# Three edits in an fp32 transformer trunk: first blocks that leave two k-tiles to the end, the sigmoid ahead of the squares, values in thirds of 344 columns

## The chip, the cores and the metric

The kernel runs on one core of a Trainium2 chip. The time is device microseconds of one execution, and a kernel's time is the median over several. TensorE (PE) multiplies matrices, VectorE (DVE), ScalarE (ACT) and GpSimd (POOL) work element by element, and SyncE (SP) issues nearly all transfers. Each engine takes its instructions strictly in the order in which the program gives them to it.

## The reference

Two layers over 256 tokens of width 1024. A layer is a half-step SwiGLU feed-forward, a token mixer, a second half-step SwiGLU, and a gated embedding; layer 0 mixes with latent attention (MLA), layer 1 with forgetting attention (FoX). Cut to what matters here:

```python
for i in range(DEPTH):
    h = h + 0.5 * swiglu(rms_norm(h, ffn_norm[i, 0]), ffn_w_in[i, 0], ffn_w_out[i, 0])
    u = rms_norm(h, mix_norm[i])
    h = h + (mla_mixer(u, ...) if i % 2 == 0 else fox_mixer(u, ...))
    h = h + 0.5 * swiglu(rms_norm(h, ffn_norm[i, 1]), ffn_w_in[i, 1], ffn_w_out[i, 1])
    gate = sigmoid(rms_norm(h, ple_norm[i]) @ ple_w_gate[i])
    h = h + gate * (p[i] @ ple_w_proj[i])
return rms_norm(h, final_norm)
# fox_mixer: q, k, v (8 heads of 128) and 8 forget logits f = u @ w_in;
# scores = q k^T / sqrt(128) + cum_q - cum_k with cum = cumsum(log_sigmoid(f + b)); causal softmax; @ w_o
```

## The kernel before, in words

Activations are kept transposed: `hT` (in the tile `state`) has 8 k-tiles of 128 features by 256 tokens. All operands of a product are split into a high and a low part (`whi`, `wlo` for weights, a pair `u` for activations), and a product is three partial ones. A feed-forward block for one k-tile is therefore two matmuls: one of 512 columns (line 235: high weights against both parts) and one of 256 (line 236: low weights against the high part). A block has 8 k-tiles.

**Weights.** The class `Weights` walks one list of tiles, `plan`. `fetch` has SP load tiles up to four ahead of the last finished one. `high` (line 97) has ACT make `whi`, `low` (line 101) has DVE make `wlo`, a 128x1024 subtraction. `pump` finishes one tile, `catch_up` pumps only if fewer than four tiles are finished ahead of those handed out (`loaded < got + 4`), and `get` hands out. Where a pump stands in the program decides where its line-101 subtraction stands among DVE's other instructions.

**Norms.** While a stage finishes its eight output tiles, the next stage's operand is built from each: `high` (line 275, ACT; line 273, DVE for the last), `low` (line 280, DVE), `square` (line 286, ACT) and a running sum of the squares `acc` (line 291, POOL). `by_token` and `by_column` turn the sum into scale factors later: two small matmuls (`pst`), a DVE operation `v`, a power on POOL (`rtok`), and two more small matmuls (`pb`). The products run on the unscaled operand, so a stage can begin before its scale is known.

**First blocks.** `blocks` starts a stage on the first k-tiles of two blocks. Before the change it runs seven k-tiles of the gate block `pg`, seven of the up block `pu`, and then the eighth of each. It is used at the start of three feed-forwards (after MLA, after the gated embedding, after FoX) and at the start of MLA.

**Gated embedding** (`ple`, between layer 0 and layer 1). For each of 8 tiles d, PE makes `ps`; DVE scales it (`zg`, line 792); ACT makes the sigmoid `sg` (line 793); DVE makes `low` of tile d-1 (line 280), perhaps a weight's `wlo` (line 101), the product `ge` (line 801) and the new `state` (line 802); ACT makes `high` and `square` of tile d, and POOL adds the square to `acc`.

**FoX.** First come the values, with the 8 forget logits beside them: four column groups `pv`, the first 264 wide, the others 256 wide, each for two token halves, 8 k-tiles and 3 partial products (lines 220 to 222). `by_token`, `by_column` and the forget gate's steps (`gates`) hang on fixed places in that loop. Then `attention` runs its heads as a pipeline: in round h it makes the shares of head h-2 (`inv`, `pr`, lines 447 to 449, DVE), the two projections of head h (`ps`, then `two` and `kqv`, lines 757 and 758), turns head h-2 (`pt`, line 455, PE), scores head h-1 (`psc`) and multiplies head h-2's values (`po`, line 462). A `catch_up` follows the second projection. From round 8 on there are no projections, and PE fills in with the output product on as many k-tiles as the table `FOX_FILLS` says.

Of the kernel before, what the change touches and what calls it, by code (L numbers as in the profile page):

```python
# [15 lines left out]
AF = mybir.ActivationFunctionType  # L16
# [3 lines left out]
P = 128  # L20
D = 1024
T = 256
KD = D // P
FF = 2816
KF = FF // P
H = 8
# [12 lines left out]
G_Q = 72  # L39
G_KV = 74  # L40
GAINS = 80


MLA_FILLS = {(7, 1): 2, (8, 0): 4, (8, 1): 4, (9, 0): 4, (9, 1): 4, (10, 0): 3, (10, 1): 3}
# [94 lines left out]

@with_exitstack  # L140
def trunk(ctx, tc, xT, xt, pT, pos, freq, bf, lead0, lead1, ffn_in, ffn_out, w_down, w_uq, w_ukv, mla_o,
          fox_qk, fox_v, fox_f, fox_o, ple_gate, ple_proj, ple_rows, gain_row, out):
    nc = tc.nc
    const = ctx.enter_context(tc.tile_pool(name="const", bufs=1))
    wp = ctx.enter_context(tc.tile_pool(name="wp", bufs=1))
# [7 lines left out]
    plan = []  # L153
# [18 lines left out]
    plan_ffn(1)  # L172
    plan_ple()
    plan_ffn(2)
    plan.extend(fox_f[c] for c in range(2))
    plan.extend(fox_v[c] for c in range(KD - 2))
    plan.extend(fox_qk[c] for c in range(2 * H))
    plan.extend(fox_o[d] for d in range(KD))
    plan_ffn(3)
# [3 lines left out]

    state = const.tile([P, GAINS + KD * T], F32, name="state")
    g_sb, hT = state[:, :GAINS], state[:, GAINS:].rearrange("p (k t) -> p k t", k=KD)

# [15 lines left out]
    def tmp(name):  # L202
        return work.tile([P, T], F32, name=name, tag="tmp", bufs=5)

    def bank(name, shape=(P, 2, T)):
        return psum.tile(list(shape), F32, name=name, tag="mm")

    W = Weights(nc, wp, plan)
# [43 lines left out]
    def blocks(ps, x):  # L252

        ws = W.get(len(ps))
        for ks in (range(KD - 1), range(KD - 1, KD)):
            for p, w in zip(ps, ws):
                part(p, w, x, ks, KD - 1)
        W.done(*ws)
# [296 lines left out]
    def keys_values():  # L555

        kqv = big.tile([P, 2 * KF, T], F32, name="kqv", tag="big")
        return kqv[:, :24, :], kqv[:, 24:32, :].rearrange("p (t c) n -> p t (c n)", t=2)
# [110 lines left out]
    def fox(norm, nxt):  # L669
        kq, v = keys_values()  # L670
# [46 lines left out]
            nc.vector.tensor_copy(cumq, pc.rearrange("p t h -> p h t"))  # L717


        for c in range(4):  # L720
            w = W.get(2)
            n = T + H if c == 0 else T
            pv = [bank("pv0", (P, n)), bank("pv1", (P, n))]
            for k in range(KD):
                for t in range(2):
                    a = (k % 4) * n
                    mm3(pv[t], [norm.pair[:, k, u, t * P:(t + 1) * P] for u in range(2)],
                        [u[:, a:a + n] for u in w[k // 4][1:]], k == 0, k == KD - 1)
                if (c, k) == (0, KD - 2):
                    norm.by_token()  # L730
                elif (c, k) == (1, 3):
                    norm.by_column()
                elif (c, k) == (2, 2):
                    steps = gates()
                if steps:
                    next(steps, None)
                if k % 4 == 3:
                    W.done(w[k // 4])
                    if k == 3:
                        W.pump()  # L740
                        W.catch_up()
            for t in range(2):
                r = norm.rtok[:, t:t + 1]
                if c == 0:
                    nc.scalar.activation(zt[:, t, :].rearrange("p (j i) -> p j i", i=32)[:, :, :H],
                                         pv[t][:, T:].rearrange("p (o h) -> p o h", o=1).to_broadcast([P, 3, H]),
                                         AF.Copy, scale=r)
                nc.scalar.activation(v[:, t, c * T:(c + 1) * T], pv[t][:, :T], AF.Copy, scale=r)
            W.pump()

        def project(h, half):
            if (h, half) == (0, 1):
# [35 lines left out]
    def ple(pp, norm, nxt):  # L788
        def gated(d, z, e):
            zg, sg, ge = tmp("zg"), tmp("sg"), tmp("ge")  # L790
            src = hT[:, d, :]
            nc.vector.tensor_mul(zg, z, norm.rb)
            nc.scalar.activation(sg, zg, AF.Sigmoid)
            if d:
                nxt.low(d - 1, hT[:, d - 1, :])

            if d < 2:
                W.pump(2 - d)
            elif d < KD - 1:
                W.catch_up(3)  # L800
            nc.vector.tensor_mul(ge, e, sg)
            nc.vector.tensor_add(src, src, ge)
            if d < KD - 1:
                nxt.high(d, src)
                nxt.square(src)
            else:
                nxt.last(d, src)
                W.pump()


        es = big.tile([P, KD, T], F32, name="es", tag="big")
        for c in range(2):
            w, = W.get()
            for i in range(4):
                if i % 2 == 0:
                    pe = bank("pe")
                if (c, i) == (1, 3):
                    norm.by_column()
                part(pe[:, i % 2, :], w, pp, range(2), at=lambda k: k * 512 + i * P)
                if i % 2:  # L820
                    nc.scalar.activation(es[:, 4 * c + i - 1:4 * c + i + 1, :], pe, AF.Copy)
            W.done(w)
            if c == 0:
                norm.by_token()
            W.pump(2 - c)
        for d in range(KD):
            ps = bank("ps", (P, T))
            block(ps, norm.pair)
            gated(d, ps, es[:, d, :])
# [128 lines left out]
    for k in range(KD):  # L958
        if k % 2 == 0:
            hi, lo = W.pair()  # L960
        c = slice(k % 2 * 4 * P, (k % 2 + 1) * 4 * P)
        n0.high(k, steps[:, k, :T], vector=k == 0)

        n = 4 * P if k else 2 * P
# [145 lines left out]
    for i in range(2):  # L1110
# [6 lines left out]
        p = Embedding(i)  # L1117
# [9 lines left out]
def _cols(w, n):  # L1127

    k, m = w.shape
    return np.ascontiguousarray(w.reshape(k // P, P, m // n, n).transpose(2, 1, 0, 3)).reshape(m // n, P, -1)  # L1130


def _layout(x, p, positions, ffn_norm, ffn_w_in, ffn_w_out, mix_norm, mla_w_down, mla_q_norm, mla_w_uq,
            mla_kv_norm, mla_w_ukv, mla_w_o, fox_w_in, fox_b_f, fox_w_o, ple_norm, ple_w_gate,
            ple_w_proj, final_norm):
    a = {}
# [6 lines left out]

    g = np.concatenate([g.reshape(75, P).T, np.zeros((P, GAINS - 75), g.dtype)], axis=1)
    a["xT"] = np.ascontiguousarray(np.concatenate([g, xT], axis=1))
# [4 lines left out]
    w = ffn_w_in.reshape(4, KD, P, 2, KF, P)  # L1150
# [6 lines left out]
    w = ffn_w_out.reshape(4, KF, P, KD, P)  # L1157
    a["ffn_out"] = np.ascontiguousarray(w.transpose(0, 3, 2, 1, 4)).reshape(4, KD, P, KF * P)

    w = mla_w_down[0]  # L1160
    cq, ckv, kr = w[:, :256], w[:, 256:384], w[:, 384:]
    ks = np.concatenate([kr[:, 32:], kr[:, :32]], axis=1)
    a["w_down"] = _cols(np.concatenate([cq, ckv, kr, ks], axis=1), P)

    w = mla_w_uq[0].reshape(256, H // 2, 2, 192)
# [3 lines left out]
    w = np.concatenate([b.reshape(256, H // 2, -1) for b in (nope, rope)], axis=-1)  # L1169
    a["w_uq"] = _cols(w.reshape(256, -1), 512)  # L1170
    w = mla_w_ukv[0].reshape(P, H, 2, P)
    a["w_ukv"] = np.ascontiguousarray(w.transpose(2, 0, 1, 3)).reshape(2, P, D)
    a["mla_o"] = _cols(mla_w_o[0], P)
    w = fox_w_in[0]
    hd = H * P
    qk = w[:, :2 * hd].reshape(D, 2, H, P).transpose(0, 2, 1, 3).reshape(D, 2 * hd)
    a["fox_qk"] = _cols(qk, P)

    v = w[:, 2 * hd + T:3 * hd].reshape(2, KD // 2, P, 3, T)
    a["fox_v"] = np.ascontiguousarray(v.transpose(3, 0, 2, 1, 4)).reshape(KD - 2, P, D)  # L1180
    f = np.concatenate([w[:, 2 * hd:2 * hd + T], w[:, 3 * hd:]], axis=1).reshape(2, KD // 2, P, T + H)
    a["fox_f"] = np.ascontiguousarray(f.transpose(0, 2, 1, 3)).reshape(2, P, -1)
    a["fox_o"] = _cols(fox_w_o[0], P)
    a["ple_gate"] = _cols(ple_w_gate[0], P)

# [5 lines left out]


_ORDER = ["xT", "xt", "pT", "pos", "freq", "bf", "lead0", "lead1", "ffn_in", "ffn_out", "w_down", "w_uq", "w_ukv", "mla_o",
          "fox_qk", "fox_v", "fox_f", "fox_o", "ple_gate", "ple_proj",
          "ple_rows", "gain_row"]


# [18 lines left out]
```

## Time and profile before

| | |
|---|---|
| median of 3 runs | 1000.98 us (1000.59 to 1001.3) |
| the profiled execution | 1000.57 us, of which the span from first to last instruction is 998.8 us |
| PE | busy 988.1 us, 99% of the span |
| DVE, ACT, POOL | 74%, 52%, 43% |
| DMA | 182 GB/s over the span |

The span is that of one execution; what a change saves or costs in it is set against its 998.8 us, and the median of the runs lies 2.2 us above the span. In the timeline's rows the first number is the start in us from the span's start, the second the length in us; then engine, line, operation, what is written and read, and shapes. A matmul's length holds its way through the pipeline, so PE's pace is read from one start to the next.

### The profile page before, as it was taken

How to read it: one execution, taken by the hardware profiler on the slowest of the kernel's cores; microseconds unless marked ns; L12 is line 12 of the kernel's file. 1: busy time of each engine (PE TensorE's matmuls, PEld its weight loads, DVE VectorE, ACT ScalarE, POOL GpSimd, SP SyncE). 2: the span in 40 equal slices, each digit the busy share in tenths (PEclk: the TensorE clock that was granted, in tenths of full speed). 3: DMA queues.
4: the chain of work that ended last, by engine and by line, in shares of the span. 5: the costliest groups of instructions: out<-in, count | busy, mean ns of one | idle time of the engine just before them, and what ended most of it. 6: DMA issues, size and time to landing. Idle time of an engine off the chain costs nothing.

```text
span 998.8 us, 16024 instructions
## 1 busy us (share of the span) xinstructions
PE 988.1 (99%) x5940; PEld 875.7 (88%) x5940; DVE 740.9 (74%) x1053; ACT 517.0 (52%) x825; POOL 424.8 (43%) x348
## 2 busy tenths in 40 slices
PE   9999999999999999999999999999999999999997
PEld 7888888998988888889888888899889888888886
DVE  6777878676778787667778876666777778876674
ACT  7555444456555444545555544546445554544552
POOL 0777730210267765111477673211221577672120
PEclk9999999999999999999999999999999999999999
DMA  8576666551456566665366656666443566666561
GB/s 324 184 254 211 191 187 189 181 167 64 130 184 203 190 185 188 188 199 190 127 205 205 194 180 188 182 197 207 146 140 103 188 204 196 189 180 200 179 211 43
DMA packets 51676, 181.60 MB, mean 182 GB/s; under 512 B 5904, under 2 KB 6160, under 8 KB 51472
## 3 DMA queue, kind: packets, MB, share of 16 engines
q1 hardware_dynamic: 51168, 179.87, 57.7%
q8 instruction: 47, 0.77, 0.3%
q10 hardware_dynamic: 432, 0.72, 0.3%
q14 instruction: 29, 0.24, 0.1%
HBM read 179.52 MB, written 1.05 MB: 181 GB/s over the span
## 4 chain that ended last, share of the span: by engine, by line
PE 90%; DVE 4%; ACT 2%; issue 2%; DMA 1%; POOL 0%; SPq 0%; POOLq 0%; ACTq 0%; DVEq 0%
PE po L235 16%; PE pu L235 16%; PE pg L235 16%; PE po L236 8%; PE pu L236 8%; PE pg L236 8%; PE ps L235 4%; PE ps L236 2%; DVE wlo L101 1%; PE ps L220 1%; PE ps L221 1%; PE ps L222 1%; PE pv L220 1%; PE pv L222 1%; PE pv L221 1%
## 5 line engine op out<-in xcount | busy, mean ns | idle before, releaser
L101 DVE TENSOR_TENSOR wlo<-raw,whi 128x1024 fp32r<-128x1024 f32 (+2 forms) x338 | 416.5, 1240 | 17.8 <-ACT whi L97 17.6
L97 ACT ACTIVATE whi<-raw 128x1024 fp32r<-128x1024 f32 (+2 forms) x338 | 336.0, 1027 | 18.3 <-DMA raw<-in_ffn_in_dram 10.5
L331 POOL TENSOR_TENSOR gu<-two 128x256 f32<-128x256 f32 x176 | 234.6, 1334 | 118.0 <-DVE two L329 108.7
L235 PE MATMUL pg<-u,whi 128*128 128x512 f32 x702 | 251.0, 395 | 0.8 <-DVE u L280 0.7
L235 PE MATMUL pu<-u,whi 128*128 128x512 f32 x702 | 250.4, 395 | 0.0
L235 PE MATMUL po<-hs,whi 128*128 128x512 f32 x704 | 246.0, 394 | 0.0
L236 PE MATMUL pg<-u,wlo 128*128 128x256 f32 x702 | 198.1, 282 | 0.3 <-DVE wlo L216 0.3
L236 PE MATMUL po<-hs,wlo 128*128 128x256 f32 x704 | 198.4, 282 | 0.0
L236 PE MATMUL pu<-u,wlo 128*128 128x256 f32 x702 | 197.9, 282 | 0.0
L235 PEld LDWEIGHTS pg<-u,whi 128*128 128x128 f32 x702 | 131.9, 188 | 31.4 <-DVE u L280 1.7
L235 PEld LDWEIGHTS po<-hs,whi 128*128 128x128 f32 x704 | 132.3, 188 | 30.0
L235 PEld LDWEIGHTS pu<-u,whi 128*128 128x128 f32 x702 | 132.0, 188 | 29.9
L236 PEld LDWEIGHTS pg<-u,wlo 128*128 128x128 f32 x702 | 132.5, 189 | 1.3 <-DVE wlo L216 1.0
L236 PEld LDWEIGHTS po<-hs,wlo 128*128 128x128 f32 x704 | 132.8, 189 | 0.0
L236 PEld LDWEIGHTS pu<-u,wlo 128*128 128x128 f32 x702 | 132.5, 189 | 0.0
L291 POOL TENSOR_TENSOR acc<-acc,sq 128x256 f32<-128x256 f32 x42 | 45.8, 1090 | 174.1 <-ACT sq L286 173.9
L212 ACT ACTIVATE hs<-hid 128x256 fp32r<-128x256 f32 x88 | 36.8, 418 | 144.5 <-POOL hid L349 142.4
L349 POOL TENSOR_TENSOR hid<-sg,gu 128x256 f32<-128x256 f32 x88 | 106.4, 1209 | 6.9
L216 DVE TENSOR_TENSOR hs<-hid,hs 128x256 fp32r<-128x256 f32 x88 | 63.1, 717 | 49.7 <-ACT hs L212 49.7
L329 DVE TENSOR_TENSOR two<-pg,rb 128x512 f32<-128x512 f32 x88 | 60.4, 686 | 46.0 <-PE pg L236 38.2
L275 ACT ACTIVATE u<-state 128x256 fp32r<-128x256 f32 x49 | 25.0, 510 | 124.6 <-DVE state L396 104.2
L343 ACT ACTIVATE sg<-gu 128x256 f32<-128x256 f32 x88 | 36.8, 418 | 77.4 <-POOL gu L331 77.4
(258 smaller groups left out, 1199.6 us busy)
## 6 DMA issues: line engine op xcount, KB each, us to landing
raw<-in_ffn_in_dram SPq DMA_DIRECT2D x172, 512.0 KB, 4.2
raw<-in_ffn_out_dram SPq DMA_DIRECT2D x64, 512.0 KB, 3.6
raw<-in_ffn_out_dram SPq DMA_DIRECT2D x32, 384.0 KB, 3.8
raw<-in_fox_qk_dram SPq DMA_DIRECT2D x16, 512.0 KB, 3.6
raw<-in_mla_o_dram SPq DMA_DIRECT2D x8, 512.0 KB, 4.1
raw<-in_ple_gate_dram SPq DMA_DIRECT2D x8, 512.0 KB, 4.5
raw<-in_fox_o_dram SPq DMA_DIRECT2D x8, 512.0 KB, 3.4
raw<-in_ple_rows_dram SPq DMA_DIRECT2D x8, 512.0 KB, 4.7
```

The lines of the kernel that those rows point to most:

```text
L97: self.nc.scalar.activation(self.pairs[i][0][:, c], self.raws[i][:, c], AF.Copy)
L101: self.nc.vector.tensor_sub(lo[:, c], self.raws[i][:, c], hi[:, c].bitcast(F32))
L212: nc.scalar.activation(hi, src, AF.Copy)
L216: nc.vector.tensor_sub(lo, src, hi.bitcast(F32))
L235: nc.tensor.matmul(ps, hi, x[:, k], start=k == 0, stop=False)
L236: nc.tensor.matmul(ps[:, 1, :], lo, x[:, k, 0, :], start=False, stop=k == last)
L275: nc.scalar.activation(self.pair[:, b, 0, c], src[:, c], AF.Copy, scale=g)
L291: nc.gpsimd.tensor_add(new, self.acc, sq)
L329: nc.vector.tensor_mul(two, ps, norm.rb2)
L331: nc.gpsimd.tensor_add(gu[c, i], two[:, 0, :], two[:, 1, :])
L343: nc.scalar.activation(sg, gu.pop((c, 0)), AF.Silu)
L349: nc.gpsimd.tensor_mul(hid[c], gu.pop((c, 0)), gu.pop((c, 1)))
```

## The change

Three things are different.

1. `blocks` runs six k-tiles of both blocks, then the seventh of both, then the eighth of both.
2. In the gated embedding, `square` of tile d-1 is issued after the sigmoid of tile d, where it was issued before it.
3. FoX's values and logits are cut into three column groups of 344 (8 logits first, then 1024 value columns) in place of 264 + 3 x 256. The weights come as nine tiles of 1032, 1032 and 688 columns for each group, where there were two of 1056 and six of 1024. The places of `by_token`, `by_column`, the gate's steps and the pumps in that loop move with it.

```diff
+FV = (H + D) // 3
...
-    plan.extend(fox_f[c] for c in range(2))
-    plan.extend(fox_v[c] for c in range(KD - 2))
+
+    plan.extend(fox_v[c, :, a * FV:min(a + 3, KD) * FV] for c in range(3) for a in range(0, KD, 3))
...
         ws = W.get(len(ps))
-        for ks in (range(KD - 1), range(KD - 1, KD)):
+        for ks in (range(KD - 2), range(KD - 2, KD - 1), range(KD - 1, KD)):
             for p, w in zip(ps, ws):
                 part(p, w, x, ks, KD - 1)
...
-        for c in range(4):
-            w = W.get(2)
-            n = T + H if c == 0 else T
-            pv = [bank("pv0", (P, n)), bank("pv1", (P, n))]
+        for c in range(3):
+            pv = [bank("pv0", (P, FV)), bank("pv1", (P, FV))]
             for k in range(KD):
+                if k % 3 == 0:
+                    w, = W.get()
+                a = (k % 3) * FV
                 for t in range(2):
-                    a = (k % 4) * n
                     mm3(pv[t], [norm.pair[:, k, u, t * P:(t + 1) * P] for u in range(2)],
-                        [u[:, a:a + n] for u in w[k // 4][1:]], k == 0, k == KD - 1)
-                if (c, k) == (0, KD - 2):
+                        [u[:, a:a + FV] for u in w[1:]], k == 0, k == KD - 1)
+                if (c, k) == (0, 5):
                     norm.by_token()
-                elif (c, k) == (1, 3):
+                elif (c, k) == (1, 0):
                     norm.by_column()
-                elif (c, k) == (2, 2):
+                elif (c, k) == (1, 4):
                     steps = gates()
                 if steps:
                     next(steps, None)
-                if k % 4 == 3:
-                    W.done(w[k // 4])
-                    if k == 3:
-                        W.pump()
+                if k % 3 == 2 or k == KD - 1:
+                    W.done(w)
+                    W.pump()
+                    if k == 2:
                         W.catch_up()
...
-                nc.scalar.activation(v[:, t, c * T:(c + 1) * T], pv[t][:, :T], AF.Copy, scale=r)
-            W.pump()
+                nc.scalar.activation(v[:, t, c * FV + b - H:(c + 1) * FV - H], pv[t][:, b:], AF.Copy, scale=r)
...
             nc.scalar.activation(sg, zg, AF.Sigmoid)
             if d:
+
+                nxt.square(hT[:, d - 1, :])
                 nxt.low(d - 1, hT[:, d - 1, :])
...
             if d < KD - 1:
                 nxt.high(d, src)
-                nxt.square(src)
```

Lines behind the edits have numbers two or three higher in the changed kernel (101 becomes 103, 235 becomes 237, 793 becomes 795).

PE, the end of the first two blocks of the feed-forward after the gated embedding; `pg_5379` and `pu_5380` are those two blocks, `pg_5425` the block behind them, and each k-tile is one pair of rows. Before:

```order
L235 MATMUL pu_5380<-u_4951,whi_5276 128x512
L236 MATMUL pu_5380<-u_4951,wlo_5277 128x256
L235 MATMUL pg_5379<-u_4951,whi_5118 128x512
L236 MATMUL pg_5379<-u_4951,wlo_5119 128x256
L235 MATMUL pu_5380<-u_4951,whi_5276 128x512
L236 MATMUL pu_5380<-u_4951,wlo_5277 128x256
L235 MATMUL pg_5425<-u_4951,whi_5320 128x512
```

With the change:

```order
L237 MATMUL pg_5379<-u_4951,whi_5118 128x512
L238 MATMUL pg_5379<-u_4951,wlo_5119 128x256
L237 MATMUL pu_5380<-u_4951,whi_5276 128x512
L238 MATMUL pu_5380<-u_4951,wlo_5277 128x256
L237 MATMUL pg_5379<-u_4951,whi_5118 128x512
L238 MATMUL pg_5379<-u_4951,wlo_5119 128x256
L237 MATMUL pu_5380<-u_4951,whi_5276 128x512
L238 MATMUL pu_5380<-u_4951,wlo_5277 128x256
L237 MATMUL pg_5425<-u_4951,whi_5320 128x512
```

The seventh k-tile of `pg` has moved behind six k-tiles of `pu`; the eighth pair stays last.

ACT in the gated embedding, two tiles with a weight's `whi` between them. Before:

```order
L275 ACTIVATE u<-state 128x256
L286 ACTIVATE sq<-state 128x256
L793 ACTIVATE sg<-zg 128x256
L97 ACTIVATE whi<-raw 128x1024
L275 ACTIVATE u<-state 128x256
L286 ACTIVATE sq<-state 128x256
L793 ACTIVATE sg<-zg 128x256
```

With the change:

```order
L277 ACTIVATE u<-state 128x256
L795 ACTIVATE sg<-zg 128x256
L288 ACTIVATE sq<-state 128x256
L99 ACTIVATE whi<-raw 128x1024
L277 ACTIVATE u<-state 128x256
L795 ACTIVATE sg<-zg 128x256
L288 ACTIVATE sq<-state 128x256
```

The sigmoid and the square have changed places; DVE's and POOL's orders in this stage are as they were.

DVE in FoX's attention, from the second projection of the last head (`two`, `kqv`) to the shares of the head before it (`inv`, `pr`), that is from the end of round 7 into round 8. Before:

```order
L757 TENSOR_TENSOR two<-ps,rb 128x512
L758 TENSOR_TENSOR kqv<-two 128x256
L447 RECIPROCAL inv<-den 128x2
L448 TENSOR_SCALAR pr<-pr,inv 128x128
L449 TENSOR_SCALAR pr<-pr,inv 128x256
L216 TENSOR_TENSOR os<-po,os 128x256
L101 TENSOR_TENSOR wlo<-raw,whi 128x1024
```

With the change:

```order
L759 TENSOR_TENSOR two<-ps,rb 128x512
L760 TENSOR_TENSOR kqv<-two 128x256
L103 TENSOR_TENSOR wlo<-raw,whi 128x1024
L449 RECIPROCAL inv<-den 128x2
L450 TENSOR_SCALAR pr<-pr,inv 128x128
L451 TENSOR_SCALAR pr<-pr,inv 128x256
L218 TENSOR_TENSOR os<-po,os 128x256
L103 TENSOR_TENSOR wlo<-raw,whi 128x1024
```

One weight subtraction more stands between `kqv` and `inv`: the `catch_up` of round 7, which found four finished tiles ahead before and finds three now, because the values' loop ends with one finished tile fewer.

More of the change, by code (lines that the diff above doesn't have):

```diff
@@ L141, in trunk @@
 def trunk(ctx, tc, xT, xt, pT, pos, freq, bf, lead0, lead1, ffn_in, ffn_out, w_down, w_uq, w_ukv, mla_o,
-          fox_qk, fox_v, fox_f, fox_o, ple_gate, ple_proj, ple_rows, gain_row, out):
+          fox_qk, fox_v, fox_o, ple_gate, ple_proj, ple_rows, gain_row, out):
     nc = tc.nc
@@ L736, in fox @@
                     next(steps, None)
-                if k % 4 == 3:
-                    W.done(w[k // 4])
-                    if k == 3:
-                        W.pump()
+                if k % 3 == 2 or k == KD - 1:
+                    W.done(w)
+                    W.pump()
+                    if k == 2:
                         W.catch_up()
+            b = 0 if c else H
             for t in range(2):
@@ L745, in fox @@
                     nc.scalar.activation(zt[:, t, :].rearrange("p (j i) -> p j i", i=32)[:, :, :H],
-                                         pv[t][:, T:].rearrange("p (o h) -> p o h", o=1).to_broadcast([P, 3, H]),
+                                         pv[t][:, :H].rearrange("p (o h) -> p o h", o=1).to_broadcast([P, 3, H]),
                                          AF.Copy, scale=r)
-                nc.scalar.activation(v[:, t, c * T:(c + 1) * T], pv[t][:, :T], AF.Copy, scale=r)
-            W.pump()
+                nc.scalar.activation(v[:, t, c * FV + b - H:(c + 1) * FV - H], pv[t][:, b:], AF.Copy, scale=r)
         def project(h, half):
@@ L1177, in _layout @@
     a["fox_qk"] = _cols(qk, P)
[L1179 to L1182, printed above, removed]
+    a["fox_v"] = _cols(np.concatenate([w[:, 3 * hd:], w[:, 2 * hd:3 * hd]], axis=1), FV)
     a["fox_o"] = _cols(fox_w_o[0], P)
@@ L1193 @@
 _ORDER = ["xT", "xt", "pT", "pos", "freq", "bf", "lead0", "lead1", "ffn_in", "ffn_out", "w_down", "w_uq", "w_ukv", "mla_o",
-          "fox_qk", "fox_v", "fox_f", "fox_o", "ple_gate", "ple_proj",
+          "fox_qk", "fox_v", "fox_o", "ple_gate", "ple_proj",
           "ple_rows", "gain_row"]
```

## The prediction

> **What bounds the kernel now.** I read the page first, then PE's timeline around each start of a stage, then the engines that PE waits for there.
>
> ```profile
> PE 988.1 (99%) x5940; PEld 875.7 (88%) x5940; DVE 740.9 (74%) x1053; ACT 517.0 (52%) x825; POOL 424.8 (43%) x348
> PE 90%; DVE 4%; ACT 2%; issue 2%; DMA 1%; POOL 0%; SPq 0%; POOLq 0%; ACTq 0%; DVEq 0%
> ```
>
> PE is busy for 99% of the span and makes 90% of the chain that ended last. So time comes only from shorter PE work or from the few places where PE stands still. The three feed-forward starts that use `blocks`, in PE's timeline (after MLA, after FoX, after the gated embedding):
>
> ```profile
> 267.94 0.28 PE L236 MATMUL pg<-u,wlo 128*128 128x256 f32 x1
> 268.16 0.50 PE L235 MATMUL pg<-u,whi 128*128 128x512 f32 x1
> 268.50 0.28 PE L236 MATMUL pg<-u,wlo 128*128 128x256 f32 x1
> ...
> 777.44 0.28 PE L236 MATMUL pg<-u,wlo 128*128 128x256 f32 x1
> 777.78 0.51 PE L235 MATMUL pg<-u,whi 128*128 128x512 f32 x1
> 778.12 0.28 PE L236 MATMUL pg<-u,wlo 128*128 128x256 f32 x1
> ...
> 483.20 0.28 PE L236 MATMUL pg<-u,wlo 128*128 128x256 f32 x1
> 484.19 0.50 PE L235 MATMUL pg<-u,whi 128*128 128x512 f32 x1 [0.72 <-DVE u L280]
> 484.53 0.29 PE L236 MATMUL pg<-u,wlo 128*128 128x256 f32 x1
> ...
> 487.79 0.40 PE L235 MATMUL pg<-u,whi 128*128 128x512 f32 x1
> 488.19 0.39 PE L236 MATMUL pg<-u,wlo 128*128 128x256 f32 x1
> 488.41 0.39 PE L235 MATMUL pg<-u,whi 128*128 128x512 f32 x1
> ```
>
> The seventh k-tile starts late in all three, since DVE's `low` of it (line 280) comes late. To size this I need PE's pace without a wait, from the first and last rows of long runs: 41 steps of 264 columns, 48 of 256, 64 of 512.
>
> ```profile
> 667.88 0.28 PE L220 MATMUL pv<-whi,u 128*128 128x264 f32 x1
> 672.86 0.29 PE L222 MATMUL pv<-wlo,u 128*128 128x264 f32 x1
> ...
> 686.23 0.28 PE L220 MATMUL pv<-whi,u 128*128 128x256 f32 x1
> 691.89 0.39 PE L235 MATMUL ps<-u,whi 128*128 128x512 f32 x1
> ...
> 969.50 0.39 PE L220 MATMUL ps<-whi,u 128*128 128x512 f32 x1
> 984.28 0.39 PE L221 MATMUL ps<-whi,u 128*128 128x512 f32 x1
> ```
>
> That is 121.5 ns for 264 columns, 117.9 for 256 and 230.9 for 512: 113.0 ns for the second 256 columns, so 0.441 ns a column and about 5 ns for each matmul. Against it the seventh k-tile loses, in its two steps, 0.10 + 0.11 = 0.21 us after MLA, 0.22 + 0.11 = 0.33 after FoX and 0.87 + 0.11 = 0.98 after the gated embedding. There a second wait follows at 487.79, 0.17 + 0.10 = 0.27: the next block `pg` lacks its `wlo`. MLA's start shows no such gap, so the new order of `blocks` does nothing there.
>
> **The change, part by part.** *Blocks, after MLA and after FoX.* With six k-tiles of `pu` ahead of it, the seventh of `pg` comes 6 x 0.35 = 2.1 us later, more than the 0.10 and 0.22 that it waited. What could be late next is the eighth k-tile, whose place stays, and the `wlo` of the third block. In DVE's order that subtraction stands behind the last `low`:
>
> ```profile
> 270.04 1.21 DVE L101 TENSOR_TENSOR wlo<-raw,whi 128x1024 fp32r<-128x1024 f32 x1
> ...
> 779.66 1.21 DVE L101 TENSOR_TENSOR wlo<-raw,whi 128x1024 fp32r<-128x1024 f32 x1
> ...
> 486.37 1.77 DVE L101 TENSOR_TENSOR wlo<-raw,whi 128x1024 fp32r<-128x1024 f32 x1
> ```
>
> It ends at 271.25 and 780.87, and the last `low`, ahead of it, before that. PE, from the rows 268.50 and 778.12, has one more matmul and nine k-tiles of 0.349 to go to the third block, and wants its `wlo` one matmul of 0.23 later: at 272.0 and 781.6. Even 0.21 and 0.33 earlier that is 0.5 and 0.4 us behind the subtraction's end. So both waits go whole: **-0.21 and -0.33 us**. Were this cover gone, they would only move to the third block, as the next case shows.
>
> *Blocks, after the gated embedding.* Here the subtraction runs from 486.37 to 488.14, and the third block's second matmul starts at 488.19, when it is out. If only the order of k-tiles changed, PE would save 0.98 us at 483 and stand still 0.98 longer at 487: **nothing** comes from the blocks alone. It takes an earlier DVE, and that is the second edit's part.
>
> *Sigmoid ahead of the square.* One tile of the gated embedding, from ACT's, DVE's and POOL's timelines:
>
> ```profile
> 471.58 0.40 ACT L286 ACTIVATE sq<-state 128x256 f32<-128x256 f32 x1
> 471.89 0.40 ACT L793 ACTIVATE sg<-zg 128x256 f32<-128x256 f32 x1
> ...
> 471.71 0.49 DVE L280 SCALAR_TENSOR_TENSOR u<-state,u 128x256 fp32r<-128x256 f32 x1 [0.24 <-ACT u L275]
> 472.32 0.75 DVE L801 TENSOR_TENSOR ge<-es,sg 128x256 f32<-128x256 f32 x1
> 473.11 0.42 DVE L802 TENSOR_TENSOR state<-state,ge 128x256 f32<-128x256 f32 x1
> ...
> 472.06 0.73 POOL L291 TENSOR_TENSOR acc<-acc,sq 128x256 f32<-128x256 f32 x1 [1.67 <-ACT sq L286]
> ...
> 476.98 1.22 DVE L101 TENSOR_TENSOR wlo<-raw,whi 128x1024 fp32r<-128x1024 f32 x1
> 478.12 0.96 DVE L801 TENSOR_TENSOR ge<-es,sg 128x256 f32<-128x256 f32 x1
> ...
> 477.00 1.80 POOL L291 TENSOR_TENSOR acc<-acc,sq 128x256 f32<-128x256 f32 x1 [1.74 <-ACT sq L286]
> ```
>
> `ge` takes 0.75 where `state`, of the same shape, takes 0.42: it ends 0.28 after POOL's `acc` (473.07 and 472.79; 479.08 and 478.80). And `acc` takes 1.80 where it met a subtraction under way: it ends 0.68 after `ge`'s start at 478.12, 0.08 before the subtraction's end. So these operations of DVE and POOL pass one at a time, in the order in which they come. With the edit, `sg` starts 0.31 earlier (471.58), so `ge` goes right behind `low`, at 472.12, and is through at 472.54; `sq` and with it `acc` come 0.31 later, at 472.37. Now `acc` waits for `ge`, to 472.46, ends 0.68 later at 473.14, and the `state` behind `ge` ends 0.28 after that: 473.42, not 473.53. The stall moves from `ge` to `state` and leaves **0.11 us**. It repeats in tiles 2, 3, 4 and 7, which have no subtraction between `low` and `ge`. Where there is one, as at 476.98, `acc` waits for it as before, and `ge` for `acc`: nothing is won or lost. Four times 0.11 is **-0.45 us** for DVE's chain and, through the subtraction at 486.37, for PE. Ends of the range: 0, if POOL gets in ahead of `ge`, and the whole 0.98 + 0.27 = 1.25, if `state` isn't held. No row shows a `state` that met an `acc`; I take 0.45, since `state` reads two tiles just as `ge` does. The Trainium skill, SBUF — State Buffer, section "Who interferes with whom", speaks against the larger gain: a VectorE operation with two SBUF inputs and a GpSimd operation that reads SBUF exclude each other, and the first to issue keeps the port until it is through. By that rule it would be 0.45 too, and without it 1.25; the trace agrees with it for `ge` and the subtraction, at 472.79 and 478.80.
>
> *Values in thirds.* The columns are the same, 48 x 264 + 144 x 256 = 144 x 344, in 48 matmuls fewer. Before: 48 x 121.5 + 144 x 117.9 ns = 22.81 us. 344 columns cost 117.9 + 88 x 0.441 = 156.7 ns, so 144 cost 22.56: **-0.25 us**. Bounds: the rate of the 512 rows gives 155.1 ns and -0.48, that of the 256 rows 158.4 and 0. The Trainium skill, TensorE: Matmul & The Clock Gate, "Back-to-back issue gap", gives N/2.4 + 2.5 ns for a matmul; by it the 48 would save 0.12 us. Its 109 ns for 256 columns is not what the rows show (117.9), so I stay with them. What hangs on this loop keeps cover. The scale `rtok` was on POOL from here:
>
> ```profile
> 673.97 1.61 POOL L310 TENSOR_TENSOR rtok<-v,mhalf 128x2 f32<-128x2 f32 x1 [3.05 <-DVE v L308]
> ```
>
> `by_token` comes after 36 x 156.7 ns in place of 42 x 121.5, so `rtok` is ready at most 0.54 later than 675.58, at 676.1. PE wants it for `by_column` after 54 x 156.7 ns, at 676.3 at the earliest. The nine transfers in place of eight on SP bring the same bytes.
>
> *One subtraction more in round 7.* This is the part that the diff doesn't show. The values' loop ends with one finished tile fewer, so `catch_up` fires where it didn't, between `kqv` and `inv`. Before, at that place, and at an earlier head where the trace has the very order that the change makes (`kqv`, `wlo`, `inv`, `pr`, `pt`):
>
> ```profile
> 750.29 0.43 DVE L758 TENSOR_TENSOR kqv<-two 128x256 f32<-128x256 f32 x1
> 750.63 0.16 DVE L447 RECIPROCAL inv<-den 128x2 f32<-128x2 f32 x1
> 751.43 0.49 PE L455 MATMUL pt<-ident,pr 128*128 128x128 f32 x3
> ...
> 705.42 0.42 DVE L758 TENSOR_TENSOR kqv<-two 128x256 f32<-128x256 f32 x1
> 705.76 1.22 DVE L101 TENSOR_TENSOR wlo<-raw,whi 128x1024 fp32r<-128x1024 f32 x1
> 707.53 0.61 PE L455 MATMUL pt<-ident,pr 128*128 128x128 f32 x3
> ```
>
> From `kqv` to `pt` it took 2.11 us there, and PE waited for `pr`. In round 8 PE has only four k-tiles of fill ahead of `pt` and starts it 1.14 after `kqv`. With the subtraction `pt` starts at 750.29 + 2.11 = 752.40, 0.97 later, and runs 0.61 in place of 0.49: **+1.1 us**. Behind `inv` wait `pr`, then PE's `pt`, `psc` and all that follows; DVE's next work there hangs on `psc` and shifts with it, so nothing gives it back. The bounds are 0, if the subtraction comes before PE needs DVE, and 1.2, its whole length. Its `whi` is not late: ACT makes it one round ahead, at the place of this row:
>
> ```profile
> 742.94 1.06 ACT L97 ACTIVATE whi<-raw 128x1024 fp32r<-128x1024 f32 x1
> ```
>
> **The sum.** -0.21 - 0.33 - 0.45 - 0.25 + 1.1 = -0.1 us: a span of 998.7 for 998.8, and 1000.8 us for the median of 1000.98. The profiled execution took 1000.57, 0.4 below the median; the difference carries over. About 0.2%, 2.0 us, is what a measurement of this kernel can tell from no change.
>
> **The rivals.** (a) *The subtraction in round 7 is hidden.* For: DVE is busy for 74% of the span alone, so there is room. Against: the subtraction is queued behind `kqv` and ahead of `inv`, where the row at 705.76 shows no room. Then the sum is -1.24: 999.7 us, still within 0.2%. (b) *Everything is won.* (a), and `state` isn't held, and 344 columns run at the rate of 512: -0.21 - 0.33 - 1.25 - 0.48 = -2.3, 998.7 us, just faster. Against it stand the rows at 705.76, 472.32 and 686.23. (c) *Only the costs come.* The chain of the gated embedding yields nothing: -0.21 - 0.33 - 0.25 + 1.1 = +0.3, 1001.3 us. It is within my case's own bounds. (d) *Slower: 344 columns cost more than a line through 256 and 512.* The place is the 144 matmuls of the values. If each cost as much as 512 columns, that is 144 x 74 ns = 10.7 us and 1011.4. It decides from (2.0 + 0.1) / 144 = 15 ns above 156.7, at 172 ns each. Against it: 264 columns already lie on the line (121.5 for 117.9 + 8 x 0.441 = 121.4).
>
> **How the numbers follow.** My case, with (c) as its upper part, 0.81; (a) 0.09; (b) 0.05; (d) 0.05. My case alone reaches from 999.8 (the gated embedding gives 1.25, the values 0.48) to 1001.5 (both give nothing). The likeliest time is 1000.8; with (a) taken in and 0.3 for the spread of a median, the range is 999.4 to 1001.7. Faster by over 0.2%: 0.05, from (b); within: 0.90, from my case and (a); slower: 0.05, from (d).
>
> **What would show it.** In the changed profile: the seventh k-tile at the three starts without a gap; `state` long (about 0.85) and `ge` short (0.42) in the gated embedding; a wait left at the third block after it, about 0.7 us; `pv` steps of 157 ns; `pt` of round 8 waiting for `pr`, about 1 us. I would be wrong if that wait is not there (999.7), if `state` runs in 0.42, or if the `pv` steps are over 172 ns.

## The result: 2.3 us slower, with two costs that the prediction does not have

The changed kernel takes 1003.36 us (1002.09 to 1004.95, median of 20 runs), the kernel before, on the same chip, 1001.06 us (1000.25 to 1002.69, 20 runs). The ratio is 1.0023, 95% interval 1.0017 to 1.0029. The profiled execution has a span of 1000.8 us, 2.06 more than before. Forecast were 1000.8 us and no change that can be told.

First the places that the prediction names, in the trace after the change. The seventh k-tile after MLA, in PE's timeline:

```profile
269.95 0.28 PE L238 MATMUL pu<-u,wlo 128*128 128x256 f32 x1
270.07 0.39 PE L237 MATMUL pg<-u,whi 128*128 128x512 f32 x1
270.29 0.28 PE L238 MATMUL pg<-u,wlo 128*128 128x256 f32 x1
```

It comes 0.12 us behind the matmul ahead of it, with no gap. Now round 8 of FoX's attention, from DVE's and PE's timelines:

```profile
750.04 0.42 DVE L760 TENSOR_TENSOR kqv<-two 128x256 f32<-128x256 f32 x1
750.38 1.22 DVE L103 TENSOR_TENSOR wlo<-raw,whi 128x1024 fp32r<-128x1024 f32 x1
751.51 0.16 DVE L449 RECIPROCAL inv<-den 128x2 f32<-128x2 f32 x1
...
751.06 0.28 PE L238 MATMUL ps<-os,wlo 128*128 128x256 f32 x1
752.14 0.61 PE L457 MATMUL pt<-ident,pr 128*128 128x128 f32 x3 [0.81 <-DVE pr L450]
```

The subtraction stands between `kqv` and `inv`, and PE, which would have gone on 0.12 after 751.06, starts `pt` 1.08 after it: 0.96 lost. The values, from their first matmul to the one after their last:

```profile
668.00 0.32 PE L222 MATMUL pv<-whi,u 128*128 128x344 f32 x1
...
691.77 0.39 PE L237 MATMUL ps<-u,whi 128*128 128x512 f32 x1
```

That is 23.77 us where it was 24.01. And the tile of the gated embedding that the prediction worked through (DVE and POOL):

```profile
472.39 0.42 DVE L805 TENSOR_TENSOR ge<-es,sg 128x256 f32<-128x256 f32 x1
472.84 0.84 DVE L806 TENSOR_TENSOR state<-state,ge 128x256 f32<-128x256 f32 x1
...
472.64 0.75 POOL L293 TENSOR_TENSOR acc<-acc,sq 128x256 f32<-128x256 f32 x1 [1.52 <-ACT sq L288]
```

`ge` now passes in 0.42, `acc` waits for it, and `state` takes 0.84 behind `acc`, as forecast.

So what was predicted is there, and yet the sum is 2 us off. The next table cuts the traces at the first matmul of each stage (the last row runs from the start of the last matmul to the end of the span) and gives the length of each stage in us before, and how far three other executions differ from it. "in" is the `pg` and `pu` part of a feed-forward, "out" its `po` part. The run w1056 is the changed kernel with other addresses, and lead the changed kernel without the subtraction in round 7; both come below. (One execution of w1056 took 1211.47 us at a granted clock of 0.75, where every other run of this case has 0.997 to 0.999, and the ratios leave it out.)

| stage | before | after | w1056 | lead |
|---|---|---|---|---|
| ffn 0 in | 124.83 | -0.28 | +0.07 | +0.69 |
| ffn 0 out | 61.55 | +0.20 | 0.00 | +0.20 |
| MLA | 75.14 | -0.10 | -0.03 | -0.12 |
| ffn 1 in | 124.22 | -0.14 | -0.22 | -0.15 |
| ffn 1 out | 61.47 | +0.15 | 0.00 | +0.15 |
| gated embedding | 29.57 | -0.10 | 0.00 | -0.10 |
| ffn 2 in | 125.26 | +0.09 | -0.53 | -0.41 |
| ffn 2 out | 61.41 | +0.21 | 0.00 | +0.21 |
| values | 24.01 | -0.24 | -0.24 | -0.24 |
| FoX attention | 83.57 | +1.00 | +1.05 | -0.08 |
| ffn 3 in | 124.22 | -0.17 | -0.36 | -0.17 |
| ffn 3 out | 61.40 | +0.26 | +0.05 | +0.26 |
| last stage | 29.93 | +0.10 | +0.07 | +0.12 |
| last matmul to the end | 7.74 | +0.98 | +0.96 | +0.97 |

Two things stand out that no edit speaks of. The four "out" parts, in which not one matmul is different, are each 0.15 to 0.26 us longer, to the hundredth the same in after and lead. The second of them, from PE's timeline, goes from 390.17 to 451.64 before and from 389.93 to 451.56 after, 61.47 and 61.63 us (the table's 0.15 is from unrounded times):

```profile
390.17 0.40 PE L235 MATMUL po<-hs,whi 128*128 128x512 f32 x1
...
451.64 0.28 PE L220 MATMUL pe<-q,whi 128*128 128x256 f32 x1
```

```profile
389.93 0.39 PE L237 MATMUL po<-hs,whi 128*128 128x512 f32 x1
...
451.56 0.28 PE L222 MATMUL pe<-q,whi 128*128 128x256 f32 x1
```

And from the last matmul to the end it takes 0.98 us more. (The first row is no effect of the change: b_blocks and b_sig, two kernels of experiment 4 whose programs are the same up to there, differ by 1.6 us in it, +1.38 and -0.21.)

What the end waits for shows in the waits of SP's queue (what waits, for what: us in total, times, longest), and the page's DMA queues (queue, kind: packets, MB, share) have one transfer of code more within the span. Both rows before:

```profile
SPq L1210 <- DMA out_dram<-fin: 2.2, 1, 2.2
...
q14 instruction: 29, 0.24, 0.1%
```

and after:

```profile
SPq L1209 <- DMA out_dram<-fin: 3.2, 1, 3.2
...
q14 instruction: 30, 0.25, 0.1%
```

The additional one is a packet of 8192 bytes of instructions. In the kernel before the last two such packets start 8.04 and 8.16 us after the last matmul, past the end; in the changed kernel one starts at 5.85, while the last store is under way. Of that store's 128 packets of 1536 bytes the longest then takes 214 ns in place of 74, and the last starts at 6.86 in place of 6.08 (us after the last matmul).

**Theories.** A: three costs add up, round 8's wait (1.0), the weights' addresses (about 1.0: every buffer of `raw`, `whi` and `wlo` is as wide as the widest weight tile, which falls from 1056 to 1032 columns, so that all of them move), and the code transfer in the last store (0.97). Rivals: B, the pace of unchanged matmuls is one execution's drift; C, the last store is late because of its own addresses or of SP's one transfer more; D, the gains of the edits did not come.

### The profile page after: what moved, and what is told of

Same layout as the page of the kernel before. It is cut to its first block, busy times and chain, and to the rows that moved or that the text cites. A ratio compares the mean times of both kernels' runs of the same rounds, so it can differ in the third digit from the quotient of the medians.

```text
span 1000.8 us, 15933 instructions
## 1 busy us (share of the span) xinstructions
PE 988.5 (99%) x5892; PEld 872.6 (87%) x5892; DVE 740.9 (74%) x1054; ACT 516.7 (52%) x824; POOL 423.8 (42%) x348
## 3 DMA queue, kind: packets, MB, share of 16 engines
HBM read 179.52 MB, written 1.05 MB: 180 GB/s over the span
## 4 chain that ended last, share of the span: by engine, by line
PE 90%; DVE 4%; ACT 2%; issue 2%; DMA 1%; POOL 0%; POOLq 0%; SPq 0%; ACTq 0%; DVEq 0%
PE po L237 16%; PE pu L237 16%; PE pg L237 16%; PE po L238 8%; PE pg L238 8%; PE pu L238 8%; PE ps L237 4%; PE ps L238 2%; DVE wlo L103 2%; PE ps L224 1%; PE ps L223 1%; PE ps L222 1%; PE pv L222 1%; PE pv L224 1%; PE pv L223 1%
```

## Experiment 1: the addresses

The same kernels with other widths reserved for the weight tiles; no instruction differs.

```diff
-        raw = self.pool.tile([P, src.shape[-1]], F32, name="raw", bufs=self.RAW)
+        raw = self.pool.tile([P, 1056], F32, name="raw", bufs=self.RAW)[:, :src.shape[-1]]
...
-        self.pairs[self.begun] = [self.pool.tile([P, n], F32R, name=x, bufs=self.PAIRS) for x in ("whi", "wlo")]
+        self.pairs[self.begun] = [self.pool.tile([P, 1056], F32R, name=x, bufs=self.PAIRS)[:, :n] for x in ("whi", "wlo")]
```

w1056 is this in the changed kernel, b1064 the same with 1064 in the kernel before.

> The changed kernel with its weight tiles (raw, whi, wlo) reserved at 1056 columns in place of 1032, used as before; no instruction is added, removed or moved, only the addresses change back to those of the kernel before. Theory A (addresses): a feed-forward block's time hangs on the buffer its weights lie in; the blocks return to the seven times of the kernel before (2773, 2806, 2828, 2808, 2773, 2816, 2776 ns; with 1032 columns they are 2774, 2795, 2799, 2805, 2790, 2815, 2814), the drift of about 1.2 us over the feed-forwards goes, and the ratio to the kernel before falls from 1.0023 to about 1.0011 (1.0001 if the last store's extra 0.97 us hangs on addresses too). Theory B (one execution's drift): the pace of the unchanged matmuls differs from run to run; the ratio stays at 1.0023 and the block times follow no buffer.

> The kernel before with its weight tiles reserved at 1064 columns (4256 bytes) in place of 1056 (4224); no instruction changes. Theory A (addresses): each buffer gets a new block time, so the set 2773, 2806, 2828, 2808, 2773, 2816, 2776 ns is gone, and the total moves by up to 2 us in either direction. Theory B: the seven times stay and the ratio is 1.000.

Measured: w1056 1002.19 us, ratio to the kernel before 1.0012 (1.0003 to 1.0021); b1064 998.53 us, ratio 0.998 (0.9971 to 0.9989). The table's column w1056 shows the "out" parts back at the length of before (within 0.05). A block's time, from its first matmul to the next block's, as median over the 22 to 24 blocks of the four feed-forwards whose weights lie in each of the seven buffers, in ns; in brackets how far `whi` and `wlo` start past the activations `u`, modulo 256 bytes, by the start addresses in the built programs:

| reserved | the seven buffers | mean |
|---|---|---|
| 1056, before and w1056 | 2773 (0, 128), 2806 (128, 0), 2827 (0, 0), 2809 (128, 128), 2773 (0, 128), 2816 (128, 0), 2776 (0, 128) | 2797 |
| 1032, after | 2774 (64, 32), 2795 (96, 64), 2799 (128, 128), 2803 (160, 160), 2790 (192, 96), 2815 (224, 192), 2810 (0, 224) | 2798 |
| 1064, b1064 | 2776 (64, 160), 2776 (224, 64), 2813 (128, 128), 2776 (32, 32), 2787 (192, 224), 2787 (96, 192), 2778 (0, 96) | 2785 |

The times belong to the buffers: the same in feed-forwards 1 to 3, with either buffer of `u` and whichever PSUM bank the block writes, mostly to 3 ns. With 1056 columns feed-forward 0 agrees too. With 1032 and 1064 it does not for all: there the buffers follow one another in another order, and (64, 32) takes 2805 ns in place of 2774, (0, 96) 2814 in place of 2778, block after block. Before, for instance, two blocks one after the other in the third feed-forward take 2.83 and 2.81 us, two later ones 2.78 and 2.77:

```profile
525.31 0.40 PE L235 MATMUL pu<-u,whi 128*128 128x512 f32 x1
...
528.14 0.40 PE L235 MATMUL pg<-u,whi 128*128 128x512 f32 x1
...
530.95 0.39 PE L235 MATMUL pu<-u,whi 128*128 128x512 f32 x1
...
533.72 0.39 PE L235 MATMUL pg<-u,whi 128*128 128x512 f32 x1
...
536.50 0.39 PE L235 MATMUL pu<-u,whi 128*128 128x512 f32 x1
...
539.27 0.39 PE L235 MATMUL pg<-u,whi 128*128 128x512 f32 x1
```

Theory B falls: the pace follows the layout, by up to 2% in this table, and the change moved the layout. That cost about 1.0 us by the rows (0.77 in the "out" parts, 0.27 in the "in" parts of feed-forwards 1 and 3, and small gains elsewhere; over all stages, the trace of lead is 0.98 longer than that of w1056_lead, which is lead with 1056 columns). The two pairs of ratios with and without 1056 columns give 1.1 and 1.5. The table's distances are counted from `u`; whether that distance counts, the address itself, or the distance between `whi` and `wlo`, was not tested apart.

**Which address matters?** Two more layouts in the kernel before, both with 1088 columns (4352 = 17 x 256 bytes) for `whi` and `wlo`, so that all seven buffers lie alike modulo 256. b_apart has 128 bytes of padding behind each group (the two lines with `pad_` below), b_same none. To make room, FoX's `cum` shares the buffer of an earlier stage's tile.

```diff
+    def tile(self, x, n):
+        t = self.pool.tile([P, 1088], F32R, name=x, bufs=self.PAIRS)[:, :n]
+        if not self.begun:
+            self.pool.tile([P, 32], F32, name="pad_" + x)
+        return t
...
-        self.pairs[self.begun] = [self.pool.tile([P, n], F32R, name=x, bufs=self.PAIRS) for x in ("whi", "wlo")]
+        self.pairs[self.begun] = [self.tile(x, n) for x in ("whi", "wlo")]
...
-        cum = work.tile([G, T], F32, name="cum", bufs=1)
+        cum = work.tile([G, T], F32, name="cum", tag="c2", bufs=1)
```

> The kernel before, no instruction changed; the tiles whi and wlo are reserved at 1088 columns (4352 bytes, 17 x 256), with 128 bytes of padding behind each group, so that in units of 256 bytes every whi starts at the same place as the activations u and every wlo 128 bytes past it. In the kernel before three of the seven buffers lie so (block times 2773, 2773, 2776 ns), in the changed kernel none. Theory (the distance of whi and wlo from u modulo 256 bytes sets a block's time): all seven buffers give 2773 to 2776 ns, mean 2774 in place of 2797. The run with 1064 columns gave 12 ns less a block and 2.2 us less span, so 23 ns less are worth 4.2 us: about 996.5 us, ratio 0.996. Rival (the time hangs on each buffer's whole address, not on this distance): seven new times between 2770 and 2830, ratio 0.997 to 1.003.

> As the run with padding, but without it: every whi and every wlo starts at the same place as u in units of 256 bytes. In the kernel before one buffer of seven lies so, and its blocks are the slowest, 2827 ns. Theory (distance modulo 256): all seven give about 2827 ns, 30 ns above the mean of the kernel before: 5.5 us more, about 1006.5 us, ratio 1.0055. Rival (whole address): seven times between 2770 and 2830, ratio 0.997 to 1.003.

Measured: b_apart 1000.84 us, ratio 0.9994 (0.9985 to 1.0003); b_same 1006.21 us, ratio 1.0055 (1.0037 to 1.0074). In b_apart all seven buffers give 2800 ns, in b_same all seven a median of 2830, though there every third block, whatever its buffer, takes 2819. Seven blocks in the third feed-forward take 19.60 us in the one and 19.79 in the other, PE's timeline of b_apart and of b_same:

```profile
522.59 0.40 PE L241 MATMUL pg<-u,whi 128*128 128x512 f32 x1
...
542.19 0.40 PE L241 MATMUL pu<-u,whi 128*128 128x512 f32 x1
```

```profile
521.48 0.40 PE L239 MATMUL pg<-u,whi 128*128 128x512 f32 x1
...
541.27 0.40 PE L239 MATMUL pu<-u,whi 128*128 128x512 f32 x1
```

So when all buffers lie alike modulo 256 bytes they are equally fast, though their whole addresses differ: that half of the theory holds, and the block times and the median of b_same came out as forecast. The other half fails: (0, 128) gave 2773 among mixed neighbours and gives 2800 alone, and before, the two buffers at (128, 0) gave 2806 and 2816. The distance from `u` is not all of it. Nor does the layout fix the time of b_same: its seven runs go from 1001.91 to 1010.31 us, where those of b_apart stay within 1.6. Its trace is of the run of 1008.79; by an estimate from these rows, 30 ns in some 264 blocks (176 and the "out" parts of 22 blocks' length each) are 8 us, so in the run of 1001.91 most blocks cannot have taken 2830. What else counts stays open.

## Experiment 2: the subtraction in round 7

```diff
                 nc.scalar.activation(v[:, t, c * FV + b - H:(c + 1) * FV - H], pv[t][:, b:], AF.Copy, scale=r)
+        W.pump()
```

One more tile is finished after the values' loop, so `catch_up` has nothing to do between `kqv` and `inv`. The run lead is that alone, w1056_lead has 1056 columns reserved as well.

> The changed kernel with one more pump at the end of the values' loop, so that the subtraction of a weight tile between kqv and inv in round 7 is made earlier, ahead of the first projection. Theory (the subtraction costs PE its whole wait): the wait of pt in round 8 (0.97 us) goes, the time falls by 1.0 to 1.1 us against the changed kernel, ratio to the kernel before 1.0012. Rival (hidden): pt waits for something else in its place or PE loses the time later, ratio 1.0023; a third way: the earlier subtraction delays the first projection's two and costs as much there.

> Both at once: weight tiles reserved at 1056 columns, and the one pump more. Theory A and the subtraction's price together: the feed-forwards' drift of 1.2 us and the 1.1 us of round 8 are both gone, what is left of the change are its gains of about 0.9 us (blocks, thirds): ratio 0.999 to 1.000, 1.0000 if the last store still lands 1 us late. If neither matters: 1.0023.

Measured: lead 1002.69 us, ratio 1.0016 (1.0007 to 1.0025); w1056_lead 1000.92 us, ratio 1.0001 (0.9993 to 1.001). In the trace of lead, DVE and PE at round 8:

```profile
750.71 0.42 DVE L760 TENSOR_TENSOR kqv<-two 128x256 f32<-128x256 f32 x1
751.05 0.16 DVE L449 RECIPROCAL inv<-den 128x2 f32<-128x2 f32 x1
...
751.73 0.28 PE L238 MATMUL ps<-os,wlo 128*128 128x256 f32 x1
751.85 0.49 PE L457 MATMUL pt<-ident,pr 128*128 128x128 f32 x3
```

`pt` follows its neighbour by 0.12, with no wait, and FoX's attention goes from +1.00 to -0.08. The earlier subtraction costs nothing that the rows show. The pairs of ratios give 0.7 and 1.1 us for it, the rows 1.08.

## Experiment 3: the code transfer in the last store

VectorE's program has 1474 instructions before and 1476 after the change (the traces show two fewer each). act_copies is the changed kernel with four of them given to ScalarE; b_plus2 is the kernel before with two more.

```diff
-                nc.vector.tensor_copy(twice[a, b], ident[a, a])
+                nc.scalar.activation(twice[a, b], ident[a, a], AF.Copy)
```

```diff
     nc.vector.memset(warm, 0.0)
+    for _ in range(2):
+        nc.vector.memset(ready, 0.0)
```

> The changed kernel with four 64x64 copies of the first feed-forward (the tile twice) made by ScalarE in place of VectorE, so that VectorE's program has four instructions fewer (two fewer than in the kernel before). Theory (code loading): in the changed kernel VectorE's last 8192 bytes of code are fetched 5.7 us after the last matmul, while the last store is under way, and its packets end 0.8 us later; with fewer instructions the fetch comes after the end as before, from the last matmul to the end it takes 7.74 us in place of 8.71, and the time falls by 0.97 us, ratio 1.0013. Rival (the last store is late because of the addresses of the output or of the tile fin, or because of SP's one transfer more): 8.71 us stay, ratio 1.0023.

> The kernel before with two more 128x2 memsets on VectorE at the very start; nothing else. Theory (code loading): VectorE's last code fetch moves into the last store, from the last matmul to the end it takes 8.71 us in place of 7.74, and the time rises by 0.97 us, ratio 1.0010. Rival (not the number of VectorE's instructions): 7.74 us stay, ratio 1.000.

Measured: act_copies 1001.87 us, ratio 1.001 (1.0001 to 1.0019), 7.86 us from the last matmul to the end; b_plus2 1001.37 us, ratio 1.0003 (0.9994 to 1.0012), 8.65 us. SP's wait for the last store in act_copies, and in b_plus2:

```profile
SPq L1209 <- DMA out_dram<-fin: 2.3, 1, 2.3
```

```profile
SPq L1212 <- DMA out_dram<-fin: 3.1, 1, 3.1
```

and the DMA view of the last 1.6 us of the store in b_plus2, by queue, where act_copies shows no q14:

```profile
DMA  9897979979986250030000030000110110100000
...
q10 hardware_dynamic: 120, 0.16, 29.0%
q1 hardware_dynamic: 30, 0.04, 6.7%
q14 instruction: 1, 0.01, 1.2%
```

The row of digits has a thin tail after the burst, which looks like packets that stand behind the code; the trace doesn't say on which DMA engine. Two memsets at the very start of the program bring 0.91 us to its end, and four instructions fewer take 0.85 away: the transfer goes with the length of VectorE's program, and theory C falls. It holds in every trace of this case: the five kernels with 1476 instructions of VectorE have the packet in the last store, the nine with 1474 or 1472 don't. Of the two ratios, 1.0010 was expected for b_plus2 and 1.0003 came, with 1.0010 within its interval; here the traces carry the verdict, not the times. The Trainium skill, Runtime: NRT & Kernel Launch, section "Instruction fetch mechanics", says that an engine streams its instructions through a DMA queue of its own and that crossing a block is mostly hidden. This one, in the last store, was not hidden; the other code transfers were not followed.

## Experiment 4: the first two edits, each alone

b_blocks is the kernel before with only the new order of k-tiles in `blocks`, b_sig with only `square` behind the sigmoid; addresses and VectorE's count stay.

```diff
-        for ks in (range(KD - 1), range(KD - 1, KD)):
+        for ks in (range(KD - 2), range(KD - 2, KD - 1), range(KD - 1, KD)):
```

```diff
             if d:
+                nxt.square(hT[:, d - 1, :])
                 nxt.low(d - 1, hT[:, d - 1, :])
...
-                nxt.square(src)
```

> The kernel before with the first edit alone (six k-tiles of both blocks, the seventh of both, the eighth of both); addresses and the number of VectorE's instructions stay. By the prediction's terms: 0.21 us less after MLA, 0.33 less after FoX, nothing after the gated embedding, where the 0.98 us only move to the third block; together 0.54 us less span, ratio 0.9995. Rival: the gated embedding gains on its own as well, then 1.0 to 1.5 us less.

> The kernel before with the second edit alone (the sigmoid ahead of the square); addresses and the number of VectorE's instructions stay. By the prediction's term VectorE's chain ends 0.45 us earlier and the second feed-forward of the layer's start waits 0.45 us less, in the state that lies behind acc: 0.45 us less span, ratio 0.9995. Rival (the wait only moves from ge to state, no gain): 0.0 us.

Measured: b_blocks 1000.41 us, ratio 0.9994 (0.9984 to 1.0003); b_sig 1000.31 us, ratio 0.9995 (0.9986 to 1.0004). The times alone show neither; the stages do. b_blocks: ffn 1 in -0.22, ffn 2 in +0.01, ffn 3 in -0.33. At the start of feed-forward 2 its wait has moved, as forecast, to the eighth k-tile and to the third block, PE's timeline of b_blocks:

```profile
487.46 0.28 PE L236 MATMUL pu<-u,wlo 128*128 128x256 f32 x1
488.01 0.50 PE L235 MATMUL pg<-u,whi 128*128 128x512 f32 x1 [0.27 <-DVE u L280]
...
488.81 0.40 PE L235 MATMUL pg<-u,whi 128*128 128x512 f32 x1
489.68 0.39 PE L236 MATMUL pg<-u,wlo 128*128 128x256 f32 x1 [0.47 <-DVE wlo L101]
```

b_sig: ffn 2 in -0.54. This one row must be read with care, though: b_plus2, which changes nothing there, has -0.37. With the sigmoid edit, five executions have -0.41 to -0.56 (lead, act_copies, w1056, w1056_lead, b_sig), and only the first profile of the changed kernel +0.09. DVE's chain in the gated embedding tells the two apart. From the end of the second tile's `state` to the end of the eighth's it takes 16.82 us before and 16.28 in b_sig, DVE's timeline of the two:

```profile
468.30 0.43 DVE L802 TENSOR_TENSOR state<-state,ge 128x256 f32<-128x256 f32 x1
...
485.12 0.43 DVE L802 TENSOR_TENSOR state<-state,ge 128x256 f32<-128x256 f32 x1
```

```profile
468.38 0.43 DVE L802 TENSOR_TENSOR state<-state,ge 128x256 f32<-128x256 f32 x1
...
484.20 0.89 DVE L802 TENSOR_TENSOR state<-state,ge 128x256 f32<-128x256 f32 x1
```

Without the edit it is 16.83 in b_blocks and 16.81 in b_plus2, with it 16.28 in w1056 and 16.25 in the first profile of the changed kernel. So the edit's gain of 0.54 is there in that profile too. What differs comes ahead of it: the second `state` ends 17.58 us after the stage's first matmul there, 17.09 before and in w1056, 16.73 in b_plus2. In the first profile of the changed kernel a weight came late, ACT's timeline there and in w1056:

```profile
463.02 1.06 ACT L99 ACTIVATE whi<-raw 128x1024 fp32r<-128x1024 f32 x1 [0.40 <-DMA raw<-in_ple_gate_dram]
464.28 1.06 ACT L99 ACTIVATE whi<-raw 128x1024 fp32r<-128x1024 f32 x1 [0.20 <-DMA raw<-in_ple_gate_dram]
```

```profile
462.52 2.00 ACT L99 ACTIVATE whi<-raw 128x1024 fp32r<-128x1024 f32 x2
```

Theory D falls: all three edits gain. Why the transfer was late in that execution was not tried.

## Experiment 5: the repairs together

best is the changed kernel with 1064 columns reserved, the pump of lead and the copies of act_copies. best_u has instead 1088 columns for `whi` and `wlo`, with padding of 96 bytes behind each group (24 columns where b_apart has 32, and `cum` as there).

> The changed kernel with the three repairs together: weight tiles reserved at 1064 columns (the pace measured with it in the kernel before was 12 ns a block and 2.2 us of span better), one more pump at the values' end (round 8's wait of 1 us goes), four small copies made by ScalarE in place of VectorE (the last code fetch comes after the end, 0.97 us). With 1056 columns and the pump alone the ratio was 1.0001. Theory (the three add up): 1.0001 less 0.0022 less 0.0009, ratio 0.997, about 998 us; from the last matmul to the end 7.74 to 7.86 us; block times as in the run with 1064 columns. Rival (the layout's gain needs the former values' tiles, or the repairs overlap): 0.999.

> The same as the run before it, but with whi and wlo at 1088 columns (17 x 256 bytes), every whi 64 bytes and every wlo 160 bytes past u in units of 256 bytes. With 1064 columns one buffer of seven lies so and gives 2776 ns. Theory 1 (this distance alone sets the time): 2776 ns in all seven buffers, 9 ns below the mean with 1064 columns, 1.6 us better than the run before it, ratio 0.995. Theory 2 (the time also hangs on how the neighbouring tiles lie, as in the run in which all seven lay like the best and all took 2800 instead of 2773 ns): one time for all seven, but another one, 2780 to 2820 ns, ratio 0.996 to 1.003.

Measured: best 997.62 us, ratio 0.9966 (0.9953 to 0.9978); best_u 993.83 us, ratio 0.9931 (0.9919 to 0.9944), 7.4 us faster than the kernel before and, by the ratios, 9.2 faster than the change as it was made. In best_u all seven buffers give 2773 ns, the fastest seen in any layout. Seven blocks of its third feed-forward take 19.42 us, where the rows of b_apart gave 19.60:

```profile
520.88 0.39 PE L243 MATMUL pu<-u,whi 128*128 128x512 f32 x1
...
540.30 0.39 PE L243 MATMUL pg<-u,whi 128*128 128x512 f32 x1
```

Theory 1 was right here in the block time, but since it failed in b_apart, this is a lucky hit and no rule: (64, 160) alone gives 2773, (0, 128) alone 2800, (0, 0) alone 2830. Its gain was forecast too small, a ratio of 0.995.

## Why the prediction was wrong

Every term of its sum came out within 0.1 us; two terms were missing. The terms as the prediction has them, and what they measured at the addresses of before (w1056, and the single edits):

| term | predicted | measured |
|---|---|---|
| blocks after MLA | -0.21 | -0.22 |
| blocks after FoX | -0.33 | -0.36 (alone -0.33) |
| blocks after the gated embedding, alone | 0 | +0.01 |
| sigmoid ahead of the square | -0.45 | -0.53 (alone -0.54, as in DVE's chain) |
| values in thirds | -0.25 | -0.24 |
| subtraction in round 7 | +1.1 | +1.05 |
| code transfer in the last store | none | +0.97 |
| addresses of the weight tiles | none | about +1.0 |

- **Subtraction in round 7.** Right, in place, mechanism and size; rival (a) fell in experiment 2, since the wait was PE's in full.
- **Sigmoid.** Right in mechanism: the stall went from `ge` to `state`, 0.42, 0.75 and 0.84 us for `ge`, `acc` and `state`. The rule of the Trainium skill, SBUF — State Buffer, section "Who interferes with whom", that VectorE and GpSimd pass one at a time there, fits these rows too. The four tiles that the prediction names gave 0.12, 0.11, 0.16 and 0.15 in b_sig where it had 0.11 each. The wait at the third block was left as forecast: in w1056 its second matmul starts 0.86 behind the first, 0.63 over PE's pace.
- **Values.** 23.77 us for 24.01; rival (d) would have needed 172 ns a matmul, and the median step of the 144 is 157 (its time, 1011.4 in the prediction, adds up to 1011.5).
- **The steps that failed.** First, the part on the values ends on "The nine transfers in place of eight on SP bring the same bytes": it took the new tiles to be alike but for their count. They are narrower at the widest, 1032 columns for 1056, that width is what every weight buffer is spaced by, and with the spacing changed the pace of matmuls that the edits never touch: about 1.0 us. Second, the sum ends at PE's last matmul and takes the 7.7 us behind it as given, and no rival had a place there. Two VectorE instructions more, 1476 for 1474, put a code transfer into the last store: 0.97 us.
- **The claim "slower: 0.05".** It rested on (d) as the only slower case. The range was made of the bounds of listed terms alone, with 0.3 us for the spread of a median, and left nothing for what the change moves without naming it.

Added up, -0.22 - 0.36 - 0.53 - 0.24 + 1.05 = -0.3, and with 0.97 and 1.0 it is +1.7 us; the medians differ by 2.3, with an interval from 1.7 to 2.9. The sum lies at its lower end; where the other 0.6 us come from stays open.

## What to carry to other kernels

When a change alters the widest tile of a pool, or the number of instructions of an engine, compare the stages that it does not touch: a difference there that repeats to 0.01 us in several executions is the change's too. A kernel whose PE is 99% busy can have more to win in where its weights lie than in its last waits (here 3.8 us between best and best_u, by the layout alone, against 1.35 by all gains of the three edits). And look at what happens after the last matmul: here nothing hid it.

## What was not expected of the hardware

- A feed-forward block of 16 matmuls took 2773 to 2830 ns with no instruction changed, by where the weight tiles lay; with all buffers alike modulo 256 bytes, every buffer gave the same median (2800, 2830, 2773 ns in three layouts). In the slowest layout the time of the whole kernel also differed by 8 us from run to run, which stays unexplained. The Trainium skill, TensorE: Matmul & The Clock Gate, section "Step-by-step: what each phase is for", says that the next weights load through a read port of their own, without taking bandwidth from the running matmul. Nothing here measures bandwidth, but where the weights lay was not indifferent. Which mechanism links them wasn't shown.
- A packet of 8192 bytes of code during the last store, there or not there by two instructions of VectorE, went with an end 8.65 to 8.72 us after the last matmul in the five traces that have it, and 7.74 to 7.87 in the nine that don't.
